# Second feed-forward product of a two-layer trunk: running sums kept in PSUM, four results in place of seven

## The chip, the core and the metric

The kernel runs on one core of one Trainium2 chip. The metric is device time in microseconds of one execution, as the median of several. The core has a matrix engine (TensorE, PE in the profile, with its weight loads as PEld), a vector engine (VectorE, DVE), a scalar engine (ScalarE, ACT), GpSimd (POOL) and a queue engine (SyncE, SP). TensorE writes to PSUM, which has 8 banks of 128 partitions x 512 fp32 numbers; VectorE and ScalarE read it. Each engine works through its own instructions in order and waits on semaphores for the others.

## The reference

Two layers on x of 512 tokens x 1024, each of attention and a feed-forward part, then a last norm:

```python
for l in range(DEPTH):                      # DEPTH = 2
    h = rmsnorm(x, attn_norm[l])
    proj = jnp.einsum('bsd,de->bse', h, w_in[l])
    ...
    x = x + jnp.einsum('bse,ed->bsd', mixed, w_o[l])
    h = rmsnorm(x, mlp_norm[l])
    u = jnp.square(jax.nn.relu(jnp.einsum('bsd,df->bsf', h, w_ff1[l])))     # 1024 -> 4096
    x = x + jnp.einsum('bsf,fd->bsd', u, w_ff2[l])                          # 4096 -> 1024
return rmsnorm(x, final_norm)
```

## The kernel before, in words

Every fp32 matrix is split into two parts, `hi` (rounded by ScalarE) and `lo` (the rest, by VectorE), and every product of two matrices is three matmuls, hi x hi, lo x hi and hi x lo (`three`, lines 261 to 266). The time goes in this order: attention of layer 0 (to about 243 us), feed-forward of layer 0 (to 569), the opening of layer 1 and its attention (to 812), feed-forward of layer 1 (to the end).

A feed-forward part runs over four groups of hidden columns (`for g in range(GROUPS)`, line 999), and each group holds two stages. The **first product** (lines 1002 to 1036) and the **second product** (lines 1037 to 1117) are both computed by a scheme of the Strassen kind: a 2 x 2 block product with seven block products and sums of blocks before and after. The first has seven steps named 1, 2, 5, 6, 7, 3, 4 (`HALVES`); it ends in activations F0 to F4. The second has seven steps, the `FORMS` 11, 21, x1, 22, x2, x3, x4. For each form:

- `roll` (line 906) splits one of the F tiles into Ah and Al, which are the stationary side of the matmuls. It is called two forms ahead; there are two buffers.
- `W.next("f")` hands out two weight units (128 x 1024 each, c = 0 and 1), each split into whi (ScalarE, line 122) and wlo (VectorE, line 123). `_Weights` keeps four pairs of such buffers in this part, so the split runs at most four units ahead.
- 24 matmuls of 512 columns go to two PSUM banks (r = 0 and 1, the two blocks of 128 tokens in one half of the tokens), in the order c, i, r: the banks take turns every three matmuls, and both are complete at the form's end (lines 1038 to 1052).
- `gather` (line 923) copies (first group, ScalarE) or adds (later groups, VectorE, line 929) both banks to that form's place in the SBUF tile Y, which has seven places of 128 x 1024.

The seven sums of products are put together in the last group only, in SBUF: `merge` (line 936) adds one place to another with an accumulating DMA from POOL's queue, `join` (line 933) does it on VectorE, `settle` (line 949) scales a result with its row factor r2 (on ScalarE in layer 0; on VectorE, with x turned by four transpositions added, in layer 1), and `add_to` (line 958) adds a scaled bank or place to a result. The result has four quarters, (token half i, column half j), each of two row blocks tb = 2i + r.

The weights of forms x1, x2, x3 and x4 are sums of weight blocks, made by DMA in HBM-to-SBUF accumulating transfers (`grow`, line 784, issued from POOL as line 789). `then` (line 792) ties each such DMA to the split of an earlier unit in the same buffer: the DMA for x4 is issued when x2's unit of the same c has been split; that for x2 when x1's has.

After the last form, layer 0 turns its result back (`back`, line 963: four transpositions on PE, an addition to x on VectorE, then `make_h`, one ScalarE and one VectorE instruction) and starts the first two products of layer 1 (`p`, lines 1129 to 1141). Layer 1 takes squares of its results (`square`), the root (`root`: VectorE, then a power on POOL), weighs with the norm's gains (`weigh`, or in `store`) and writes eight pieces of the output from SP's queue (line 992).

The order of instructions on each engine is that of a scheduler which fills in by priority, close to the order in which the code is written; `behind` (line 239) fixes one instruction after another. The bank tags are t (2 banks), mm (2), s (3) and o (1).

## Time and profile before

| | |
|---|---|
| median of 3 runs | 1148.61 us (1148.3 to 1149.41) |
| the profiled execution | 1148.57 us, of which the span from the first to the last instruction is 1146.5 us |
| TensorE busy | 1119.3 us, 98% of the span, 6834 matmuls |
| VectorE, ScalarE, GpSimd busy | 924.4, 722.1, 181.0 us |
| mean granted clock | 0.992 |

"L123" in a row is line 123 of the kernel. A group's row reads: line, engine, operation, what it writes <- what it reads, shapes, count. A row of a timeline reads: start, us, engine, line, operation, names, shape, count, and in brackets the engine's idle time just before it with what ended it. Names lose their buffer numbers, and the forms x1 to x4 all read as "x"; "f" are the banks of the first product, "q" and "yw" raw weights.

### The profile page before, as it was taken

To read this page: it belongs to the slowest core of one execution; us is meant where nothing else is said; L and a number is where in the kernel's file an instruction comes from. 1 tells how busy PE (TensorE), PEld (TensorE's weight loads), DVE (VectorE), ACT (ScalarE), POOL (GpSimd) and SP (SyncE) were. 2 spreads that over 40 slices of the span, in tenths; PEclk is the share of its full clock that TensorE was granted. 3 is DMA by queue.
4 is the path that set the end of the run, shared out by engine and by line. 5 is a ranking of instruction groups with operands and counts; after the bars stand their busy time and mean duration, and the time that the engine had idled before them with its cause. 6 is when DMAs were issued, how large, how long until landed. Compare 5 with 4: busy or idle time off the path is not lost.

```text
span 1146.5 us, 18089 instructions
## 1 busy us (share of the span) xinstructions
PE 1119.3 (98%) x6834; PEld 996.3 (87%) x6834; DVE 924.4 (81%) x1235; ACT 722.1 (63%) x1137; POOL 181.0 (16%) x261
## 2 busy tenths in 40 slices
PE   9999999999999999999899999999999999999995
PEld 6889989899899899898688898888998998988984
DVE  6898678898877878778869976887988788798697
ACT  6456666667867557565445566665678574675664
POOL 1001432110110201102000024231102011021022
PEclk9999999999999999999899999999999999999998
DMA  7664443346976885978416743524469859778595
GB/s 250 174 181 140 126 133 111 102 120 182 219 184 173 191 233 128 220 219 177 98 55 184 215 117 111 161 78 165 75 201 208 219 129 210 210 146 212 149 182 138
DMA packets 61479, 187.07 MB, mean 163 GB/s; under 512 B 7632, under 2 KB 8656, under 8 KB 61392
## 3 DMA queue, kind: packets, MB, share of 16 engines
q1 hardware_dynamic: 46416, 131.88, 36.2%
q0 software_dynamic: 14832, 54.01, 26.8%
q8 instruction: 54, 0.88, 0.3%
q14 instruction: 33, 0.27, 0.1%
q10 hardware_dynamic: 144, 0.02, 0.0%
HBM read 154.95 MB, written 2.10 MB: 137 GB/s over the span
## 4 chain that ended last, share of the span: by engine, by line
PE 82%; DVE 6%; issue 4%; DMA 3%; ACT 3%; POOL 1%; SPq 0%; POOLq 0%; ACTq 0%; DVEq 0%
PE f L264 8%; PE f L265 8%; PE f L266 8%; PE x L266 4%; PE x L264 4%; PE x L265 4%; PE wo L264 3%; PE wo L266 2%; PE wo L265 2%; DVE wlo L123 2%; DMA q<-in_w 2%; ACT whi L122 1%; PE T0s L539 1%; PE T1s L539 1%; PE v0w L264 1%
## 5 line engine op out<-in xcount | busy, mean ns | idle before, releaser
L123 DVE TENSOR_TENSOR wlo<-q,whi 128x1024 fp32r<-128x1024 f32 x184 | 223.3, 1221 | 69.5 <-ACT whi L122 69.3
L122 ACT ACTIVATE whi<-q 128x1024 fp32r<-128x1024 f32 x184 | 194.3, 1056 | 116.4 <-PE f L265 37.4
L266 PE MATMUL f<-T_hi,wlo 128*128 128x256 f32 x512 | 145.1, 283 | 0.7 <-DVE wlo L123 0.7
L264 PE MATMUL f<-T_hi,whi 128*128 128x256 f32 x512 | 145.0, 283 | 0.0
L265 PE MATMUL f<-T_lo,whi 128*128 128x256 f32 x512 | 144.9, 283 | 0.0
L264 PE MATMUL f<-h_hi,whi 128*128 128x256 f32 x384 | 109.7, 286 | 1.4 <-DVE F L896 1.4
L789 POOL DMA_DIRECT2D q<-in_w x64 | 56.3, 933 | 338.3 <-DVE wlo L123 306.3
L266 PE MATMUL f<-h_hi,wlo 128*128 128x256 f32 x384 | 108.6, 283 | 0.0
L265 PE MATMUL f<-h_lo,whi 128*128 128x256 f32 x384 | 108.6, 283 | 0.0
L264 PE MATMUL x<-whi,Ahx 128*128 128x512 f32 x256 | 100.9, 394 | 1.6 <-ACT Ahx L223 1.6
L266 PE MATMUL x<-whi,Alx 128*128 128x512 f32 x256 | 100.6, 393 | 1.3 <-DVE Alx L224 1.3
L265 PE MATMUL x<-wlo,Ahx 128*128 128x512 f32 x256 | 100.1, 391 | 0.0
L266 PEld LDWEIGHTS f<-T_hi,wlo 128*128 128x128 f32 x512 | 98.3, 192 | 1.1 <-DVE wlo L123 1.1
L264 PEld LDWEIGHTS f<-T_hi,whi 128*128 128x128 f32 x512 | 98.3, 192 | 0.0
L265 PEld LDWEIGHTS f<-T_lo,whi 128*128 128x128 f32 x512 | 98.3, 192 | 0.0
L123 DVE TENSOR_TENSOR wlo<-raw,whi 128x1024 fp32r<-128x1024 f32 (+1 forms) x68 | 79.2, 1171 | 7.7 <-ACT whi L122 7.6
L122 ACT ACTIVATE whi<-raw 128x1024 fp32r<-128x1024 f32 (+1 forms) x68 | 66.2, 982 | 29.7 <-PE p1d1q L265 5.3
L264 PEld LDWEIGHTS f<-h_hi,whi 128*128 128x128 f32 x384 | 73.5, 191 | 2.7 <-DVE F L896 1.8
L265 PEld LDWEIGHTS f<-h_lo,whi 128*128 128x128 f32 x384 | 73.6, 192 | 0.3
L266 PEld LDWEIGHTS f<-h_hi,wlo 128*128 128x128 f32 x384 | 73.6, 192 | 0.0
L264 PEld LDWEIGHTS x<-whi,Ahx 128*128 128x128 f32 x256 | 48.5, 189 | 11.9 <-ACT Ahx L223 2.0
L266 PEld LDWEIGHTS x<-whi,Alx 128*128 128x128 f32 x256 | 48.4, 189 | 11.8 <-DVE Alx L224 1.7
(965 smaller groups left out, 3108.7 us busy)
## 6 DMA issues: line engine op xcount, KB each, us to landing
q<-in_w SPq DMA_DIRECT2D x100, 512.0 KB, 4.6
q<-in_w POOLq DMA_DIRECT2D x84, 512.0 KB, 6.7
raw<-in_w SPq DMA_DIRECT2D x62, 512.0 KB, 3.7
yw<-in_w SPq DMA_DIRECT2D x12, 512.0 KB, 5.5
yw<-in_w POOLq DMA_DIRECT2D x12, 512.0 KB, 8.3
cs<-in_w SPq DMA_DIRECT2D x8, 512.0 KB, 7.5
ww<-in_w SPq DMA_DIRECT2D x8, 512.0 KB, 4.3
Y<-Y POOLq DMA_DIRECT2D x6, 512.0 KB, 6.1
```

What stands on the lines that cost most here:

```text
L122: h = nc.scalar.activation(hi[:, a:b], raw[:, a:b], AF.Copy)
L123: self.last = h, nc.vector.tensor_tensor(out=lo[:, a:b], in0=raw[:, a:b], in1=hi[:, a:b].bitcast(F32), op=ALU.subtract)
L264: nc.tensor.matmul(pt, ah, bh, start=first, stop=False, skip_group_check=onto)
L265: nc.tensor.matmul(pt, ah, bl, start=False, stop=False, skip_group_check=onto)
L266: nc.tensor.matmul(pt, al, bh, start=False, stop=last, skip_group_check=onto)
L539: nc.tensor.transpose(pt[:, n * P : (n + 1) * P], u["w"][qi][:, kb * P : (kb + 1) * P], ident)
L789: paced(nc.gpsimd.dma_start(t, quad(g, q, c), accum_op=ALU.add))
```

## The change

`TAPS` gives each form a chain and one of the four quarters. Form 11 opens chain r, 21 opens s, x1 opens t; 22 adds on to t's two banks, and x2, x3 and x4 add on to r's, whose sums so stay in PSUM from form 11 to the group's end. After every form the two banks, running sums by then, are read into the quarter that the form feeds: copied in the first group where it is the first to feed it, otherwise added. Y shrinks from seven places to four, and no merges, joins or copies between places are left. Within a form the loop is now r, c, i: all 12 matmuls of row block 0, its read, then those of row block 1. The row factor of layer 0 is applied in the last group as before; in layer 1 the factor is left out, and instead x, scaled with its inverse, is added to the quarters (`lay`) during the first products of groups 1 and 2, with the epsilon of the last norm scaled to match.

The place freed in SBUF goes to a fifth pair of split weights (pool f2 with three buffers, `pairs`), so the split runs up to five units ahead in the first product; in the second it is called four units ahead at a form's start and once more after its reads, and set behind them.

```diff
+TAPS = {"11": ("r", 1, 0), "21": ("s", 1, 0), "x1": ("t", 0, 1), "22": ("t", 1, 1),
+        "x2": ("r", 1, 1), "x3": ("r", 0, 1), "x4": ("r", 0, 0)}
...
+        if _UNITS[i][0] in "fq":
+            for x, y in zip(self.last, before):
+                self.behind(x, y)
+    def pairs(self):
+        return 3 * len(self.pools) - 1
...
-            self.do_split(i + 2 * len(self.pools), i)
+            self.do_split(i + self.pairs() - less, i)
...
-            Y = fp.tile([P, len(FORMS), 2, 512], F32, tag="Y", name=f"Y{l}")
+            Y = fp.tile([P, 2, 2, 2, 512], F32, tag="Y", name=f"Y{l}")
...
+            def gather(i, j, r, pt):
+                o = place(2 * i + r, j)
+                if 2 * i + j in fresh:
+                    nc.scalar.copy(o, pt)
+                    if r:
+                        fresh.discard(2 * i + j)
+                else:
+                    return nc.vector.tensor_add(o, o, pt)
...
+            def lay(tb, j):
+                o = place(tb, j)
+                n = 24 * j + tb
+                nc.vector.scalar_tensor_tensor(
+                    out=o, in0=turned(tb, j), scalar=fin[:, n : n + 1], in1=o, op0=ALU.mult, op1=ALU.add)
...
+                            if last and g in (1, 2) and q in "5673":
+                                lay("5673".index(q), g - 1)
+                chains = {}
                 for f, form in enumerate(FORMS):
+                    chain, i, j = TAPS[form]
+                    fresh_bank = chain not in chains
+                    if fresh_bank:
+                        chains[chain] = [bank(("s", "s", "s", "mm", "mm", "o")[2 * len(chains) + r], f"{form}{l}{g}{r}")
+                                         for r in range(2)]
+                    to = chains[chain]
+                    us = [W.next("f", 1 + c) for c in range(GP // 2)]
+                    hi, lo = rolled[form]
+                    for r in range(2):
+                        for n, (c, e) in enumerate((c, e) for c in range(GP // 2) for e in range(2)):
+                            at = 512 * c + 256 * e + r * P
+                            three(to[r], (hi[:, at : at + P], lo[:, at : at + P]), wpair(us[c], e, 512),
+                                  fresh_bank and n == 0, n == 3, not fresh_bank)
+                        tb = 2 * i + r
+                        if end and not last and form in ("21", "x2", "x3", "x4"):
+                            tapped = add_to(tb, j, to[r])
+                        else:
+                            tapped = gather(i, j, r, to[r])
...
+                            if form == "x4":
+                                for c_ in CAME[2 * r : 2 * r + 2]:
+                                    back(c_)
+                        elif form in ("21", "x2", "x3", "x4"):
+                            square(tb, j)
+                            if form in ("x2", "x4"):
+                                root(tb)
+                            if form in ("21", "x3"):
+                                weigh(tb, j)
+                            elif form == "x2":
+                                weigh(tb, 1)
+                                store(tb, 0, True)
+                                store(tb, 1, True)
+                            elif form == "x4":
+                                store(tb, 0, False)
+                                store(tb, 1, True)
                     if f + 2 < len(FORMS):
                         roll(FORMS[f + 2])
+                    if f + 1 < len(FORMS):
+                        had = W.split
+                        W.do_split(W.used + 3, W.used)
+                        if W.split > had and tapped:
+                            behind(W.last[1], tapped)
```

Left out of it are the removed lines of merges, joins and the old endings, and the place of the tile vs, which moves to a pool that is given back when attention ends.

How the instructions stand is shown at three places. The first is VectorE in group 1 of layer 0, forms x2 to x4. In the order before, from the roll (Alx) of x3 on: wlo are splits of weights, Alx rolls, and Y rows additions of a bank (first those of 22, then of x2, then of x3).

```order
L224 TENSOR_TENSOR Alx_4260<-F_2674,Ahx_4259 128x1024
L123 TENSOR_TENSOR wlo_4268<-q_0_2669,whi_4267 128x1024
L123 TENSOR_TENSOR wlo_4285<-q_0_2666,whi_4284 128x1024
L929 TENSOR_TENSOR Y_2860<-Y_2860,x_4265 128x512
L929 TENSOR_TENSOR Y_2860<-Y_2860,x_4266 128x512
L224 TENSOR_TENSOR Alx_4303<-F_2676,Ahx_4302 128x1024
L123 TENSOR_TENSOR wlo_4311<-q_0_2667,whi_4310 128x1024
L123 TENSOR_TENSOR wlo_4329<-yw_2862,whi_4328 128x1024
L929 TENSOR_TENSOR Y_2860<-Y_2860,x_4308 128x512
L929 TENSOR_TENSOR Y_2860<-Y_2860,x_4309 128x512
L123 TENSOR_TENSOR wlo_4349<-yw_2863,whi_4348 128x1024
```

The same place in the changed order, from the reads of 22 on (x_4178 and x_4179 are the banks of chain t, 11010 and 11011 those of chain r). Line numbers are the changed kernel's: 127 is the split, 234 the roll, 941 the addition.

```order
L941 TENSOR_TENSOR Y_2868<-Y_2868,x_4178 128x512
L941 TENSOR_TENSOR Y_2868<-Y_2868,x_4179 128x512
L127 TENSOR_TENSOR wlo_4255<-q_0_2672,whi_4254 128x1024
L234 TENSOR_TENSOR Alx_4251<-F_2678,Ahx_4250 128x1024
L127 TENSOR_TENSOR wlo_4260<-q_0_2673,whi_4259 128x1024
L941 TENSOR_TENSOR Y_2868<-Y_2868,11010_4098 128x512
L941 TENSOR_TENSOR Y_2868<-Y_2868,11011_4099 128x512
L127 TENSOR_TENSOR wlo_4295<-q_0_2670,whi_4294 128x1024
L234 TENSOR_TENSOR Alx_4291<-F_2680,Ahx_4290 128x1024
L127 TENSOR_TENSOR wlo_4301<-q_0_2671,whi_4300 128x1024
L941 TENSOR_TENSOR Y_2868<-Y_2868,11010_4098 128x512
L941 TENSOR_TENSOR Y_2868<-Y_2868,11011_4099 128x512
```

Before, a form's two reads stand together behind one or two splits that they do not depend on, and nothing on PE needs them soon. Now a split, a roll and a split stand between the second read of one form and the first read of the next, and the reads of x2 and x3 are from the banks that the next form adds to.

The second place is ScalarE in the last group of layer 0, from x2's roll to x3's. Before (L956 scales a result, L122 splits a weight, L223 rolls):

```order
L223 ACTIVATE Ahx_5711<-F_2675 128x1024
L122 ACTIVATE whi_5719<-q_0_2667 128x1024
L956 ACTIVATE Y_2860<-Y_2860,fin 128x512
L122 ACTIVATE whi_5736<-q_0_2668 128x1024
L956 ACTIVATE Y_2860<-Y_2860,fin 128x512
L223 ACTIVATE Ahx_5752<-F_2674 128x1024
L122 ACTIVATE whi_5761<-q_0_2669 128x1024
L122 ACTIVATE whi_5779<-q_0_2666 128x1024
```

and in the changed order (954 scales, 125 splits, 233 rolls):

```order
L125 ACTIVATE whi_5699<-q_0_2671 128x1024
L954 ACTIVATE Y_2868<-Y_2868,fin 128x512
L233 ACTIVATE Ahx_5690<-F_2679 128x1024
L954 ACTIVATE Y_2868<-Y_2868,fin 128x512
L125 ACTIVATE whi_5736<-q_0_2672 128x1024
L125 ACTIVATE whi_5740<-q_0_2673 128x1024
L954 ACTIVATE Y_2868<-Y_2868,fin 128x512
L233 ACTIVATE Ahx_5732<-F_2678 128x1024
```

Before, the first scaling reads a place that an accumulating DMA from POOL's queue writes. In POOL's order of that group before, L937 are those DMAs, Y to Y, among the weights' DMAs:

```order
L789 DMA q_0_2666<-in_w 128x1024
L937 DMA Y_2860<-Y_2860 128x1024
L789 DMA q_0_2667<-in_w 128x1024
L789 DMA q_0_2668<-in_w 128x1024
L789 DMA q_0_2669<-in_w 128x1024
L937 DMA Y_2860<-Y_2860 128x1024
L789 DMA q_0_2666<-in_w 128x1024
L789 DMA q_0_2667<-in_w 128x1024
L937 DMA Y_2860<-Y_2860 128x1024
```

In the changed order the scalings read places that VectorE has added to, and POOL's queue there holds weights' DMAs alone.

The third place is VectorE at the end of the program. Before, from the additions (L960) into the first quarter on; L977 is the first half of a root, L982 and L990 weigh:

```order
L960 SCALAR_TENSOR_TENSOR q_1_8430<-Y_8620,fin,q_1_8430 128x512 x2
L960 SCALAR_TENSOR_TENSOR Y_8620<-Y_8620,fin 128x512 x2
L960 SCALAR_TENSOR_TENSOR Y_8620<-x_11654,fin,Y_8620 128x512
L982 TENSOR_TENSOR Y_8620<-Y_8620,cs 128x512 x2
L977 TENSOR_SCALAR fin<-fin 128x1
L960 SCALAR_TENSOR_TENSOR Y_8620<-x_11655,fin,Y_8620 128x512
L990 SCALAR_TENSOR_TENSOR Y_8620<-Y_8620,fin,cs 128x512
L982 TENSOR_TENSOR q_1_8430<-q_1_8430,cs 128x512
L977 TENSOR_SCALAR fin<-fin 128x1
L990 SCALAR_TENSOR_TENSOR Y_8620<-Y_8620,fin,cs 128x512
```

In the changed order, from x3's reads on (941 adds a bank, 981 is the root's half, 986 and 994 weigh):

```order
L941 TENSOR_TENSOR Y_8590<-Y_8590,11130_11339 128x512
L941 TENSOR_TENSOR Y_8590<-Y_8590,11131_11340 128x512
L986 TENSOR_TENSOR Y_8590<-Y_8590,cs 128x512 x2
L941 TENSOR_TENSOR Y_8590<-Y_8590,11130_11339 128x512
L981 TENSOR_SCALAR fin<-fin 128x1
L994 SCALAR_TENSOR_TENSOR Y_8590<-Y_8590,fin,cs 128x512
L941 TENSOR_TENSOR Y_8590<-Y_8590,11131_11340 128x512
L981 TENSOR_SCALAR fin<-fin 128x1
L994 SCALAR_TENSOR_TENSOR Y_8590<-Y_8590,fin,cs 128x512
```

The additions of scaled places and of two banks with their factor are gone; what stands behind PE's last bank is one read, half a root and one weighing.

More of the change, by code (lines that the diff above doesn't have):

```diff
@@ L116, in split_part @@
             self.turn = k + 1
-            hi = self.pools[k // 2].tile([P, 1024], F32R, tag="whi", name=f"whi{i}")
-            lo = self.pools[k // 2].tile([P, 1024], F32R, tag="wlo", name=f"wlo{i}")
+            pool = self.pools[k > 1]
+            hi = pool.tile([P, 1024], F32R, tag="whi", name=f"whi{i}")
+            lo = pool.tile([P, 1024], F32R, tag="wlo", name=f"wlo{i}")
             self.tiles[i] = (hi, lo)
@@ L143, in do_split, with next @@
                 fn()
-    def next(self, kind):
+    def next(self, kind, less=0):
         i = self.used
@@ L241, in behind @@
             mybir.DependencyClass.NoSync, mybir.DependencyReason.DATA), reason="order")
+    W.behind = behind
     def rms_a(src, inv_n, col, name, floor=None):
@@ L1034, in trunk @@
                                 less(3, 1, 3)
-                            if end and q in "56":
-                                settle("56".index(q), 0)
+                            if last and g in (1, 2) and q in "5673":
+                                lay("5673".index(q), g - 1)
+                chains = {}
                 for f, form in enumerate(FORMS):
-                    to = [bank((("s", "s"), ("s", "mm"), ("mm", "o"))[f % 3][r], f"{form}{l}{g}{r}") for r in range(2)]
-                    work = [(c, i, r) for c in range(GP // 2) for i in range(2) for r in range(2)]
@@ new lines, in trunk @@
+                    for r in range(2):
[6 more added lines that the diff above has]
+                            tapped = add_to(tb, j, to[r])
+                        else:
+                            tapped = gather(i, j, r, to[r])
+                        if not end:
+                            continue
+                        if not last:
+                            if form in ("11", "x1", "22"):
+                                settle(tb, j)
+                            if form == "x1":
+                                settle(r, 0)
+                            if form == "x4":
[14 more added lines that the diff above has]
+                                store(tb, 1, True)
@@ L1131, in trunk @@
                 pts = [bank("mm", f"p{l + 1}{i}") for i in range(2)]
-                for tb in (0, 1):
-                    add_to(tb, 0, to[tb])
-                for c in CAME[2:4]:
-                    back(c)
                 for n, c in enumerate(CAME):
```

136 lines of the change are left out of this document (19 added, 117 removed).

## The prediction, made before the changed kernel ran

> **What bounds it now.** I read PE's share first, then the table of stages, then TensorE's own timeline for places where it stood still.
>
> ```profile
> PE 1119.3 (98%) x6834; PEld 996.3 (87%) x6834; DVE 924.4 (81%) x1235; ACT 722.1 (63%) x1137; POOL 181.0 (16%) x261
> 323.00:364.00 41.00, 41.00 (x343) 40.87 (x342) 29.41 (x30) 27.37 (x37) 3.50 (x4) 1.00 0.69 182
> 364.00:402.00 38.00, 38.00 (x170) 31.47 (x169) 33.39 (x36) 21.68 (x22) 7.12 (x8) 1.00 0.83 187
> 521.10:583.50 62.40, 57.26 (x250) 45.41 (x248) 52.31 (x63) 33.43 (x42) 8.07 (x11) 0.95 0.55 116
> 1090.80:1133.30 42.50, 41.32 (x194) 33.52 (x192) 38.10 (x45) 23.61 (x33) 9.77 (x13) 1.00 0.81 162
> ```
>
> The columns of a stage are its stretch, its length, then busy us (and instructions) of PE, PE's weight loads, DVE, ACT and POOL, then the granted clock, the DMA share and GB/s. The first stage is the first product of group 1 in layer 0, the second that group's second product. PE is busy in all of both: the middle of a feed-forward part is TensorE's own time, and removing DVE, ACT or DMA work there gains nothing. The third stage (last second product of layer 0 and the opening of layer 1) holds 5 us in which PE is not busy, at a mean clock of 0.95; the fourth is the last second product. The change keeps the number of matmuls and transposes, so it can gain only where PE stands still: here, behind PE's end, and at the two starts of a feed-forward part.
>
> ```profile
> 363.98 0.40 PE L264 MATMUL 11010_4097<-whi,Ah 128*128 128x512 f32 x1
> 396.64 0.39 PE L264 MATMUL x<-whi,Ahx 128*128 128x512 f32 x1
> ```
>
> These are the first matmuls of products 11 and x4 of one group, six products of 24 matmuls apart: 32.66 / 144 = 0.227 us a matmul, 5.45 us a product, 2.72 us for one of its two banks. This is my clock below; T is the start of a group's product 11.
>
> **Term 1, the end of layer 0.**
>
> ```profile
> 546.83 0.72 ACT L956 ACTIVATE Y<-Y,fin 128x512 f32<-128x512 f32 x1 [6.99 <-DMA Y<-Y]
> 548.11 0.39 PE L266 MATMUL x<-whi,Alx 128*128 128x512 f32 x1
> 550.12 0.50 PE L264 MATMUL x<-whi,Ahx 128*128 128x512 f32 x1 [1.62 <-ACT Ahx L223]
> 552.15 0.79 PE L266 MATMUL x<-whi,Alx 128*128 128x512 f32 x1 [1.30 <-DVE Alx L224]
> 552.74 0.63 PE L264 MATMUL x<-whi,Ahx 128*128 128x512 f32 x1
> 555.64 0.39 PE L265 MATMUL x<-wlo,Ahx 128*128 128x512 f32 x1
> 556.61 3.49 DVE L934 TENSOR_TENSOR Y<-Y 128x1024 f32<-128x1024 f32 x3
> 562.70 0.39 PE L266 MATMUL x<-whi,Alx 128*128 128x512 f32 x1
> 568.00 1.25 PE L966 MATMUL yT<-edge,Y 128*128 128x128 f32 x8 [1.89 <-DVE x L967]
> 573.55 1.03 PE L966 MATMUL yT<-edge,Y 128*128 128x128 f32 x8
> 574.34 0.71 PE L264 MATMUL p<-h_hi,whi 128*128 128x512 f32 x2
> 583.32 0.39 PE L266 MATMUL p<-h_hi,wlo 128*128 128x512 f32 x1
> ```
>
> ACT stands 6.99 us because the scaling of a result waits for a merging DMA; the roll of x3 (Ahx, Alx) is queued behind it, PE waits for both halves, and then matmuls come 0.43 us apart instead of 0.227 (552.74 on). From 548.11 to 555.64 there are 10 matmuls: 7.53 - 10 x 0.227 = 5.3 us lost. The merges and joins go with the change, so ACT has no DMA to wait for and the half-speed matmuls go too. From 562.70 to the end of the opening (583.32 + 0.23) there are 55 matmuls (12.5 us) and 32 transposes (eight take 574.34 - 573.55 = 0.79, so 3.2): 20.85 - 15.7 = 5.2 us lost, since DVE did 3.49 us of joins and then every addition to the last rows after the last matmul. Now rows 0 are added while PE computes rows 1, so two of the eight turns back come before PE's last half product. What is late next is the second weight of the opening: its split on DVE follows the last addition and two additions to x, some 3.3 us behind PE's end, while PE has 0.8 of transposes and 1.8 us of matmuls before it needs it: 0.7 us stays. The gain is 5.3 + 5.2 - 0.7 = **9.8 us**; at most 10.5, at least 5.3 if DVE is as late as now.
>
> **Term 2, the end of the kernel.**
>
> ```profile
> 1117.44 0.40 PE L266 MATMUL x<-whi,Alx 128*128 128x512 f32 x1
> 1119.02 0.66 PE L946 MATMUL xT<-edge,x 128*128 128x128 f32 x4 [1.18 <-DVE Y L952]
> 1132.93 0.39 PE L266 MATMUL x<-whi,Alx 128*128 128x512 f32 x1
> 1136.20 2.51 POOL L982 TENSOR_TENSOR q<-q,cs 128x512 f32<-128x512 f32 x1 [2.06 <-ACT F L972]
> 1138.45 0.63 ACT L972 ACTIVATE F<-Y 128x512 f32<-128x512 f32 x1
> 1138.99 0.19 ACT L972 ACTIVATION_READ_ACCUMULATOR F<-Y 128x1 f32 x1
> 1140.53 0.21 DVE L977 TENSOR_SCALAR fin<-fin 128x1 f32<-128x1 f32 x1
> 1140.81 0.54 POOL L978 TENSOR_TENSOR fin<-fin,mhalf 128x1 f32<-128x1 f32 x1 [1.59 <-DVE fin L977]
> 1141.39 0.75 DVE L990 SCALAR_TENSOR_TENSOR Y<-Y,fin,cs 128x512 f32<-128x512 f32 x1 [0.66 <-POOL fin L978]
> 1142.63 0.40 SPq L992 DMA_DIRECT2D out_xT<-q  x1
> ```
>
> PE loses 1119.02 - 1117.44 - 0.23 = 1.35 us where a transposition of x waits for a bank; these eight transpositions move into the first products of groups 1 and 2, where they cost PE what they cost it now. Behind PE's end (1133.32) the last output leaves at 1142.63: 9.3 us, in which one row block waits for a 2.5 us product on POOL and for DVE to work off four additions. After the change one addition (0.7), square and sum (0.75), root on DVE to POOL's start (0.3), power (0.55), weighing (0.8) and the second output's issue (0.45) are left: 3.6 us, plus 0.2 for the first reader and 0.4 because rows 0's weighing stands before it on DVE. That is 4.2, a gain of 5.1 + 1.35 = 6.5 us. Against it stand the weighings and squares that now come inside products 21, x2 and x3 (term 4): 1.6 us of waits. Net **4.9 us**, between 3 and 6.5.
>
> **Term 3, the starts of the first product.**
>
> ```profile
> 263.98 0.39 PE L266 MATMUL f<-T_hi,wlo 128*128 128x256 f32 x1 [0.33 <-DVE wlo L123]
> 273.61 0.39 PE L264 MATMUL f<-h_hi,whi 128*128 128x256 f32 x1 [0.72 <-DVE F L896]
> 832.84 0.38 PE L266 MATMUL f<-T_hi,wlo 128*128 128x256 f32 x1 [0.39 <-DVE wlo L123]
> 842.41 0.38 PE L264 MATMUL f<-h_hi,whi 128*128 128x256 f32 x1 [0.69 <-DVE F L896]
> ```
>
> With five pairs of split weights in place of four, the sums over two weights, and with them the DMAs that wait for them, are one weight (2.7 us) earlier. The four waits, 2.1 us, can all go; a burst on DVE could also add 1 us. I take **1.1 us**.
>
> **Term 4, the waits that the change adds.** Products x2, x3 and x4 now add into the same two banks, 22 into those of x1. Before PE may go on, DVE must have read a bank; behind that read, in order, stand two splits and a roll.
>
> ```profile
> 525.67 1.22 DVE L123 TENSOR_TENSOR wlo<-q,whi 128x1024 fp32r<-128x1024 f32 x1
> 526.80 1.22 DVE L914 SCALAR_TENSOR_TENSOR F<-F,F 128x1024 f32<-128x1024 f32 x1
> 529.07 0.68 DVE L929 TENSOR_TENSOR Y<-Y,11030_5589 128x512 f32<-128x512 f32 x1
> 529.67 0.68 DVE L929 TENSOR_TENSOR Y<-Y,11031_5590 128x512 f32<-128x512 f32 x1
> 390.01 1.06 ACT L122 ACTIVATE whi<-q 128x1024 fp32r<-128x1024 f32 x1 [2.26 <-DMA q<-in_w]
> 393.88 1.06 ACT L122 ACTIVATE whi<-q 128x1024 fp32r<-128x1024 f32 x1 [1.64 <-DMA q<-in_w]
> DMA to landing us min/median/max: 5.2/6.8/11.4
> ```
>
> DVE's starts are 1.13 us apart for 1024 columns and 0.60 for 512. From the end of one product to the first bank of the next being read it does one read, a split, a roll, a split, a read: 0.60 + 3 x 1.13 + 0.60 = 4.6, with 0.2 for the first reader 4.8, and PE comes back after 5.45. So 0.65 us is spare and DVE alone costs nothing; in the last group of layer 1, two weighings more (1.2) make it 6.0 behind 21 and, with two roots, 6.4 behind x2, so PE waits 0.55 + 0.95, the 1.6 above.
>
> But the roll follows the splits on ACT, and the split of x4's second weight waits for its accumulating DMA. After that landing come whi 1.05, Ahx 1.0, Alx 1.13, wlo 1.13 and the read 0.6: 5.0 us, due at T + 32.7, so it may land at T + 27.7. Now it lands at 393.8 - 364.0 = T + 29.8, and PE does not mind, since it waits for no read. In the new order x2's second split, which sends that DMA, comes behind the last read of x1 (T + 16.35 + 0.2 + 0.6), a split and a roll, and ends at T + 20.5; the issue is some 0.4 later, T + 20.9. A landing after 5.2 us costs nothing, after the median 6.8 nothing either (T + 27.7), after 11.4 it costs 4.6. Group 0 has fewer DVE additions and sends it earlier, group 3 loads nothing for a next group; groups 1 and 2 of both layers are exposed. I take the median with 0.4 us of scatter, 4 x 0.4 = **1.6 us lost**, between 0 and 18.
>
> **The sum.** The profiled execution took 1148.57 us, 2.1 more than its span of 1146.5, and 0.04 below the median of the three runs. 1148.57 - 9.8 - 4.9 - 1.1 + 1.6 = 1134.4.
>
> **Rivals.**
> *The late DMA stays late* (0.22). The transfers land where they do now, up to 2.1 us after T + 27.7, and PE waits before x4 in four groups, with some half-speed matmuls behind as at 552.74: 6 to 8 us in all, 1139 to 1141. For it: ACT waits for this DMA twice in the group shown. Against: the next group's loads, which share the DMA engines then, are sent later in the new order.
> *The cover is complete* (0.12). No new wait, all of terms 1 to 3: 10.5 + 6.5 + 2.1 = 19.1, so 1129.5.
> *It does not do what it says at layer 0's end* (0.05). ACT and DVE are late there without merges as well, since every scaling still stands in ACT's queue ahead of a roll: the gain of term 1 halves, 1139 to 1143.
> *Slower: the chains bind on the DMA* (0.04). PE waits at x4 for the read of its own bank, because DVE stands behind a roll and a split whose DMA is late. Terms 1 to 3 give 15.8; in the four exposed groups the waits outweigh that from 4 us each, that is with a transfer of 10.8 us; at 11.4 in all four, 18.4 us, 1151.
> *Slower: no cover inside a product* (0.02). PE shows the read of each of three continuations in eight groups, 24 x (0.2 + 0.6) = 19 us: 1152. Against it: 0.65 us is spare at each by the rows of term 4. The Trainium skill, page "Perfetto Trace Analysis", section "Matmuls", stands behind this case: it advises that independent matmul groups rotate through different PSUM banks, so that one's evacuation overlaps the next one's matmuls, and x2, x3 and x4 no longer rotate. In the trace of before, which does rotate, no wait of PE on such a read shows, so it neither proves nor denies the rule.
>
> My forecast, 1131.5 to 1138, has 0.55. The range of 1129.5 to 1142 takes in the late DMA and half the complete cover. Faster means by over 0.2% (2.3 us, what a measurement of this kernel can tell from no change): 0.90; within it 0.04; slower 0.06.
>
> **What would show it.** Term 1: no ACT wait for a DMA of Y, PE without a gap over 1 us from 521 to the end of the opening, a clock of 1.00 there, and a stage of about 53 us in place of 62.4. Term 2: last output issued some 4 us after PE's last matmul, the last second product near 40 us. Term 4: look at PE before the first matmul of x3 and x4 for waits on the read (L941 in the changed kernel), and on ACT for a wait on a DMA before x4's split. Waits of over 2 us there in most groups would prove me wrong, as would an unchanged gap where layer 1 opens.

## The result, and the profile after

The changed kernel takes 1156.05 us (median of 4 runs, 1154.85 to 1158.56) beside 1148.45 us for the kernel before: a ratio of 1.0068, 95% interval 1.0048 to 1.0087. It is slower by 0.7%, where 1134.4 us had been forecast. The forecast's gains are nearly all there; the waits that the change adds cost about 26 us in place of some 3.

TensorE's line of the page, and the four stages that answer to those shown of before (stretch, length, busy us of PE, weight loads, DVE, ACT and POOL, granted clock, DMA share, GB/s):

```profile
PE 1122.9 (97%) x6834; PEld 995.5 (86%) x6834; DVE 921.8 (80%) x1238; ACT 712.3 (62%) x1121; POOL 172.8 (15%) x253
324.30:365.18 40.88, 40.88 (x342) 40.78 (x340) 30.29 (x31) 26.84 (x36) 3.51 (x4) 1.00 0.78 200
365.18:403.50 38.32, 37.35 (x166) 30.53 (x165) 32.29 (x35) 20.82 (x22) 7.10 (x8) 1.00 0.74 168
525.23:579.61 54.38, 53.13 (x250) 43.51 (x248) 46.11 (x56) 33.07 (x42) 5.45 (x8) 1.00 0.43 94
1099.62:1147.76 48.14, 41.33 (x170) 32.89 (x168) 34.54 (x42) 24.83 (x37) 7.70 (x9) 0.93 0.52 117
```

The end of layer 0 fell from 62.4 to 54.4 us. But the second product of group 1, which was all PE's own time, now holds 1 us in which PE stands, and the last second product grew from 42.4 to 48.1 us at a clock of 0.93. PE's timeline shows the places; these four, among them the longest, stand in front of a continuation, a product that adds on to banks in use:

```profile
393.54 0.47 PE L276 MATMUL 11010_4098<-whi,Ahx 128*128 128x512 f32 x1 [0.97 <-DVE Y L941]
553.87 0.47 PE L276 MATMUL 11030_5572<-whi,Ahx 128*128 128x512 f32 x1 [1.25 <-DVE Y L964]
1052.04 0.47 PE L276 MATMUL 11120_10603<-whi,Ahx 128*128 128x512 f32 x1 [2.25 <-DVE Y L941]
1052.81 0.63 PE L276 MATMUL 11120_10603<-whi,Ahx 128*128 128x512 f32 x1
1053.24 0.63 PE L277 MATMUL 11120_10603<-wlo,Ahx 128*128 128x512 f32 x1
1139.76 0.77 PE L276 MATMUL 11130_11339<-whi,Ahx 128*128 128x512 f32 x1 [5.50 <-ACT Y L992]
```

The banks named 110.., 111.. are those of chain r: 393.54 and 553.87 are the first matmuls of x3, 1052.04 and 1139.76 of x4. Each waits for VectorE's read of the bank to which it adds. In the groups 0 PE also stops at 21, which opens a chain and waits for its roll: 0.70 us in layer 0, 0.94 and 0.70 in layer 1. Behind the longer two, matmuls come 0.43 us apart (1052.81 to 1053.24), as at 552.74 before.

The balance by stretches (us; T is the start of a group's product 11):

| stretch | before | after | early splits (below) |
|---|---|---|---|
| to T of group 0, layer 0 | 285.0 | 284.1 | 285.0 |
| groups 0, 1, 2 of layer 0 | 79.0, 78.6, 78.6 | 81.1, 79.9, 80.2 | 81.0, 78.6, 78.6 |
| last second product and opening | 62.4 | 54.4 | 52.7 |
| attention, to T of group 0, layer 1 | 270.2 | 270.6 | 271.1 |
| groups 0, 1, 2 of layer 1 | 79.0, 78.6, 79.4 | 84.5, 81.4, 83.5 | 84.7, 80.2, 78.6 |
| last second product | 42.4 | 48.1 | 39.8 |
| behind PE's last matmul | 13.3 | 7.4 | 8.0 |

In layer 1 the stretches of groups 0 and 1 each hold 1.6 us of transpositions that moved into the first products behind them (80.15 against 78.57 us in the early version); they left the last second product.

**Why a read is late.** Group 1 of layer 0 (T = 365.18), from the split of x3's second weight on, on ACT and on DVE:

```profile
388.39 1.06 ACT L125 ACTIVATE whi<-q 128x1024 fp32r<-128x1024 f32 x1 [1.47 <-DVE Y L941]
389.36 1.05 ACT L233 ACTIVATE Ahx<-F 128x1024 fp32r<-128x1024 f32 x1
390.44 1.23 DVE L234 TENSOR_TENSOR Alx<-F,Ahx 128x1024 fp32r<-128x1024 f32 x1 [0.33 <-ACT Ahx L233]
391.58 1.22 DVE L127 TENSOR_TENSOR wlo<-q,whi 128x1024 fp32r<-128x1024 f32 x1
392.71 0.68 DVE L941 TENSOR_TENSOR Y<-Y,11010_4098 128x512 f32<-128x512 f32 x1
```

The DMA that makes x3's second weight landed at 388.29 (T + 23.1), 0.1 us before ACT's split. From there to PE's first matmul of x3 at 393.54 it is 5.25 us: whi, roll on ACT, roll and split on DVE, read. x3 was due at T + 27.2. The bank itself had been complete since about 389.9, where its last matmul of x2 ended.

**Why the transfer is late.** POOL's issues in that group:

```profile
374.72 0.90 POOL L802 DMA_DIRECT2D q<-in_w  x1 [14.05 <-DVE wlo L127]
375.86 1.79 POOL L802 DMA_DIRECT2D q<-in_w  x2 [0.24 <-DVE Y L941]
380.71 0.88 POOL L802 DMA_DIRECT2D q<-in_w  x1 [3.06 <-DMA q<-in_w]
383.96 0.90 POOL L802 DMA_DIRECT2D q<-in_w  x1 [2.37 <-DVE wlo L127]
388.42 0.89 POOL L802 DMA_DIRECT2D q<-in_w  x1 [3.56 <-DVE Y L941]
```

These are the two sums for x2, the two for x3 and the two for x4, at T + 9.5, 10.7, 11.3, 15.5, 18.8 and 23.2. They land at T + 15.2, 18.1, 20.6, 23.1, 26.1 and 28.6, some 2.5 us apart, so a late first one makes all late. The fourth, x3's second, has one more tie: it waits on POOL for the first to land (the wait for a DMA in its row) and leaves 0.3 us later, here as in groups 1 and 2 of the traces of the kernel before, early splits, half late and late sums. Before the change the first left at T + 6.2 and landed at T + 11.8.

**In the last group** more comes behind a late transfer. ACT first, then DVE:

```profile
1131.98 1.06 ACT L125 ACTIVATE whi<-q 128x1024 fp32r<-128x1024 f32 x1 [2.75 <-DMA q<-in_w]
1132.95 0.62 ACT L976 ACTIVATE F<-Y 128x512 f32<-128x512 f32 x1
1133.56 1.04 ACT L233 ACTIVATE Ahx<-F 128x1024 fp32r<-128x1024 f32 x1
1133.69 0.27 DVE L981 TENSOR_SCALAR fin<-fin 128x1 f32<-128x1 f32 x1 [4.67 <-ACT F L976]
1134.63 1.23 DVE L234 TENSOR_TENSOR Alx<-F,Ahx 128x1024 fp32r<-128x1024 f32 x1
1137.01 0.27 DVE L981 TENSOR_SCALAR fin<-fin 128x1 f32<-128x1 f32 x1
1138.93 0.68 DVE L941 TENSOR_TENSOR Y<-Y,11130_11339 128x512 f32<-128x512 f32 x1
```

x4's second weight lands at T + 32.3. The square of x2's row block stands behind its split on ACT; DVE stands 4.67 us at the root that needs the square, and the roll of x4, a second root, weighings and a split follow before the read of x3's bank at 1138.93. PE's row at 1139.76 names a scaling of Y on ACT, which no matmul reads; the read of its bank ends at the same time, 1139.6.

### The profile page after: what moved, and what is told of

Same layout as the page of the kernel before. It is cut to its first block, busy times and chain, and to the rows that moved or that the text cites. A ratio compares the mean times of both kernels' runs of the same rounds, so it can differ in the third digit from the quotient of the medians.

```text
span 1155.2 us, 18065 instructions
## 1 busy us (share of the span) xinstructions
PE 1122.9 (97%) x6834; PEld 995.5 (86%) x6834; DVE 921.8 (80%) x1238; ACT 712.3 (62%) x1121; POOL 172.8 (15%) x253
## 4 chain that ended last, share of the span: by engine, by line
PE 67%; DMA 10%; DVE 10%; issue 6%; ACT 4%; POOL 2%; SPq 0%; POOLq 0%; ACTq 0%; DVEq 0%
DMA q<-in_w 9%; PE f L276 8%; PE f L277 8%; PE f L278 8%; DVE wlo L127 3%; PE wo L276 2%; PE wo L278 2%; PE wo L277 2%; DVE Alx L234 1%; DVE Y L941 1%; ACT whi L125 1%; POOL q L802 1%; ACT Ahx L233 1%; DVE F L926 1%; PE T0s L552 1%
## 5 line engine op out<-in xcount | busy, mean ns | idle before, releaser
L234 DVE TENSOR_TENSOR Alx<-F,Ahx 128x1024 fp32r<-128x1024 f32 x32 | 39.1, 1223 | 21.9 <-ACT Ahx L233 21.8
L896 ACT ACTIVATE F<-F 128x512 f32<-128x512 f32 x48 | 29.9, 625 | 23.7 <-DVE F L902 16.3
L897 ACT ACTIVATE F<-F 128x512 f32<-128x512 f32 x64 | 40.2, 629 | 1.4
L234 DVE TENSOR_TENSOR Al<-F,Ah 128x1024 fp32r<-128x1024 f32 x24 | 29.3, 1222 | 11.0 <-ACT Ah L233 11.0
L485 POOL TENSOR_TENSOR sig1s<-sig1s,C1s 128x128 f32<-128x128 f32 (+3 forms) x32 | 26.2, 819 | 70.1 <-DVE C1s L482 55.0
```

The source lines that it names most:

```text
L234: nc.vector.tensor_tensor(out=lo, in0=src, in1=hi.bitcast(F32), op=ALU.subtract)
L485: nc.gpsimd.tensor_mul(sig[:, 0:wd], sig[:, 0:wd], C[:, 1 : wd + 1])
L896: nc.scalar.activation(f(n), f(n) if src is None else src, AF.Relu, scale=scale)
L897: nc.scalar.activation(f(n), f(n), AF.Square)
```

## The experiments

Each kernel is the changed one, or the version with early splits, with the edits shown.

### What makes PE wait

**Fresh banks.** Where PE waits for a read, does the shared bank make the wait, or the late weight itself?

```diff
-                    fresh_bank = chain not in chains
+                    fresh_bank, chain = True, "rst"[f % 3]
...
-    chains[chain] = [bank(("s", "s", "s", "mm", "mm", "o")[2 * len(chains) + r], f"{form}{l}{g}{r}")
+    chains[chain] = [bank(("s", "s", "s", "mm", "mm", "o")[2 * (f % 3) + r], f"{form}{l}{g}{r}")
```

> Every form starts in the pair of banks that was read longest ago (three pairs take turns) and adds to nothing; the order of instructions on every engine stays that of the changed kernel. Left out of the computation: the running sums over forms. Theory 1 (late weights through shared banks): in the changed kernel the second weights of x3 and x4 come late, VectorE stands behind their roll and split, so the read of a bank comes late, and PE waits only because the next form adds to that same bank. Then no wait of PE on a read (L941) is left at x3 and x4, the last second product falls from 48.1 us to about 43, and the time from 1156 to about 1141 to 1145. Theory 2 (late weights by themselves): PE would wait for the split or the roll anyway, at the same places and almost as long; 1153 to 1156.

Measured: 1144.61 us (1141.58 to 1151.31, ten runs). Two stages of it, group 1 of layer 0 and the last second product:

```profile
365.00:402.00 37.00, 37.00 (x165) 30.62 (x163) 31.59 (x35) 20.86 (x22) 6.46 (x8) 1.00 0.73 166
1090.80:1136.60 45.80, 41.54 (x169) 33.02 (x168) 34.92 (x42) 25.09 (x37) 7.68 (x9) 0.93 0.54 122
```

In the middle group PE no longer stands, with every instruction in its old order and x3's second weight as late as before (T + 22.8 to 24.6 in groups 1 and 2). So there the shared bank turns a late weight into a wait. In the last group PE still waits, 1.55 us for x4's roll and 1.9 us for a split: 45.8 us, not 43, so there the weight is late by itself too.

The Trainium skill, page "Perfetto Trace Analysis", section "Matmuls", advises that independent groups rotate through PSUM banks. This run agrees with it (11.4 us better with banks that rotate); the version with early splits shows that it isn't the whole rule, since chained banks cost nothing in its groups 1 and 2 (78.6 us).

**Single blocks.** Is it the transfers that are late, or is VectorE's queue too long in itself?

```diff
                 else:
-                    paced(nc.gpsimd.dma_start(t, quad(g, q, c), accum_op=ALU.add))
                     W.raw[_AT[("f", l, g, form, c)]] = t
```

> The changed kernel without the accumulating DMAs of the second product: each form takes the block that already lies in its place, rolls and splits it as before. Left out of the computation: the sums of weight blocks of x1, x2, x3 and x4. Theory 1 (late weights): no ACT wait on a DMA before the splits of x3 and x4, VectorE reads in time, and PE's waits at x3 and x4 vanish: middle groups lose some 9 us of waits, the last one 5 or more, 1138 to 1144. Rival (VectorE's own queue: read, split, roll, split, read is too long beside a product in itself): the waits of about 1 us at x3 and x4 of each group stay, 1150 to 1155.

Measured: 1132.66 us, less than expected.

```profile
362.47:400.20 37.73, 37.73 (x169) 31.23 (x168) 32.69 (x35) 21.51 (x22) 1.75 (x2) 1.00 0.29 79
1081.10:1121.60 40.50, 38.58 (x170) 31.17 (x168) 34.44 (x42) 24.69 (x37) 2.42 (x3) 1.00 0.13 45
```

With the same order on VectorE and nothing to wait for, all middle groups run as before the change (78.6 us, without the moved transpositions). VectorE's queue does fit beside a product, as the prediction had it; 0.8 us before 22 and 1.4 us before x4 of the last group are left. The groups 0 lose nothing either (79.0 us, and 80.6 with 1.6 of transpositions), so what they lose in the changed kernel hangs on the transfers too.

### When the sums leave

**Early splits.** The look-ahead is called at a form's start again, so that the splits of x1, and the sums that follow them, don't stand behind the reads.

```diff
-                    us = [W.next("f", 1 + c) for c in range(GP // 2)]
+                    us = [W.next("f") for c in range(GP // 2)]
...
-                    if f + 1 < len(FORMS):
-                        had = W.split
-                        W.do_split(W.used + 3, W.used)
-                        if W.split > had and tapped:
-                            behind(W.last[1], tapped)
```

> The split of the form after next's first weight is called at a form's start again, not behind its reads; still five pairs. Theory 1: x2's first accumulating DMA leaves about 5 us earlier than T + 9.5, and the four behind it with it, so that x3's second weight lands by T + 20 in place of T + 23.1 and x4's by T + 26 in place of T + 28.6 to 32.3. The waits of the middle groups go, that of the last is halved: 1141 to 1147. Rival: the transfers are limited by their own queue (2.5 us each) or by slots that PE still reads, and come hardly earlier: within 2 us of 1156; or the reads now stand behind more splits: above 1157.

Measured: 1138.60 us, ratio 0.9919 (0.9904 to 0.9934): this is faster than both kernels. x2's first sum leaves at T + 3.1 and x3's second lands at T + 18.3 to 20.2 in groups 1 and 2. Those groups lose nothing (first row), and the end of layer 0 takes 52.7 us without a stop (second):

```profile
365.97:403.80 37.83, 37.83 (x169) 31.35 (x168) 32.77 (x35) 21.74 (x22) 7.11 (x8) 1.00 0.87 189
523.10:575.80 52.70, 52.70 (x250) 43.67 (x248) 46.01 (x56) 33.03 (x42) 5.46 (x8) 1.00 0.47 98
```

**Late sums, half late.** The reverse: splits and reads stay early, and only the DMAs for x2 and x3 wait longer, by one product or by one weight.

```diff
-                    then("f", g, "x1", c, grow, g, "x2", "22", c)
+                    then("f", g, "22", c, grow, g, "x2", "22", c)                    # late sums
+                    then("f", g, "22" if c else "x1", 1 - c, grow, g, "x2", "22", c) # half late
...
-                            then("f", g, "x1", c, grow, g, "x3", "22", c_)
+                            then("f", g, "22", c, grow, g, "x3", "22", c_)           # late sums
+                            then("f", g, "22", 0, grow, g, "x3", "22", c_)           # half late
```

> The version with early splits (1138.6 us), but the accumulating DMAs for x2 and x3 are tied to the splits of 22 in place of those of x1, one product (5.45 us) later; splits, reads and rolls stand where they stood. Theory 1: x2's first sum leaves near T + 8.5 in place of T + 3.1, x3's second lands after T + 23 in place of T + 18.3 to 20.2, ACT waits for it and PE waits for the reads of x2 and x3 again, as in the changed kernel: 1146 to 1158. Rival (the place of the reads on VectorE, not the transfers, made the early version fast): within 2 us of 1138.6.

> The version with early splits, with the accumulating DMAs for x2 and x3 one weight (2.7 us) later in place of one product. Theory 1 with its bound for x3's second weight (landing by T + 22, since whi, roll, split and read behind it take 5.2 us and x3 is due at T + 27.2): it lands at T + 21 to 22.5, so PE's wait before x3 is under 0.5 us in groups 1 and 2, and the time between the early version's 1138.6 and the changed kernel's 1156, near the lower end: 1139 to 1146. Rival (cost grows in proportion to lateness, 38 us for 5.45 us): half of that, 1155 or more.

Measured: 1176.65 us for late sums and 1156.97 us for half late. Both directions were right, both sizes too small, and half late took the time that its rival had named (1155 or more). The DMA row shows what happened. It is the mean busy share of the DMA engines in 1 us slices from T of group 1 of layer 0, in tenths: first the changed kernel, then early splits, then late sums.

```profile
DMA  8582000000098999999999997999997880888999
DMA  9874739919699999999999997894757396999997
DMA  9865000000009699999999999999999935887999
```

```profile
GB/s 340 147 303 98 0 0 0 0 0 0 0 74 147 213 197 201 209 201 221 205 209 209 197 197 143 131 209 205 365 356 307 156 356 12 160 332 115 160 193 168
```

In the changed kernel and in late sums the engines stand idle from T + 4 until the first sum leaves, and are full from then on, at some 200 GB/s (the row below them is the changed kernel's), that is about 2.5 us for a weight of 512 KB. An idle stretch can't be made up. The four traces together, for groups 1 and 2 of both layers:

| | x3's second weight lands at T + | stop before x3, us |
|---|---|---|
| early splits | 20.2, 18.7, 18.3, 18.6 | none |
| half late | 22.6, 21.5, 22.4, 23.6 | 1.1, 0, 0.8, 2.0 |
| changed kernel | 23.1, 23.1, 22.8, 22.7 | 1.1, 1.1, 0.8, 0.7 |
| late sums | 24.0, 25.6, 23.6, 25.6 | 2.3, 4.1, 2.7, 4.0 |

The stop is about the landing less 22, and up to 1.1 us more in these groups, so the bound of T + 22 held there. The whole time grew in proportion all the same, as the rival had it: 18.4 us for sums sent 2.7 us later and 38 us for 5.45. What failed in the half-late forecast was the landing: it came up to 1.1 us later than expected, as late as in the changed kernel. And the first and last groups were in neither sum: the groups 0 took 85.1 and 86.0 us in half late against 81.0 and 84.7 with early splits, and its last group stood 2.7 us behind x1; in late sums the stretch at the end of layer 0 took 59.3 us.

### What else the change moved

**Late ending.** x2's squares, root, weighing and outputs behind the reads of x3, in the changed kernel; and then the same edit with early splits and four pairs of split weights (four late), and with early splits, five pairs and the shorter look-ahead of group0_four below (combined).

```diff
-                            if form in ("x2", "x4"):
-                                root(tb)
...
+                    if end and last and form == "x3":
+                        for tb in (2, 3):
+                            square(tb, 1)
+                            root(tb)
+                            weigh(tb, 1)
+                            store(tb, 0, True)
+                            store(tb, 1, True)
```

> In the last group of layer 1 squares, root, weighing and outputs of x2's two row blocks are called behind the reads of x3; nothing else is moved. Theory 3: there x4's roll and last split stand on VectorE behind two roots and weighings that wait for squares on ACT, and this makes the 5.7 us wait of PE before x4 and the half-speed matmuls behind it (2.9 us). Then PE waits about 2 us at most there, at full speed, and the end of the kernel behind PE grows by 1 us at most: 1147.5 to 1150. Rival: x4's weight, landed at T + 32.3, sets that wait, and the moved work only filled it: a wait of 3 us or more stays, the tail grows by 1 to 3 us, 1152 to 1156.

Measured: 1159.09 us (1154.04 to 1160.44), above both forecasts and not clearly apart from the changed kernel's 1154.85 to 1158.56. The edit's own place gained: the last second product took 44.5 us in place of 48.1, with 2.6 us of PE's wait before x4 left of 5.5 and the same time behind PE (7.5 us), though x4's second weight landed 0.8 us earlier in this trace (T + 31.5). But 8 matmuls at half speed came behind it, and the six groups ahead, whose instructions weren't touched, lost 3 us more in this trace than in the changed kernel's. So by these two traces the moved work made up to half of that wait and x4's late weight the rest, and the total doesn't show it.

**Four pairs.** Early splits with four pairs in place of five.

```diff
-        return 3 * len(self.pools) - 1
+        return 2 * len(self.pools)
...
-            f2 = right.enter_context(tc.tile_pool(name=f"f2{l}", bufs=3, side="right"))
+            f2 = right.enter_context(tc.tile_pool(name=f"f2{l}", bufs=2, side="right"))
```

> The version with early splits, with four pairs of split weights as before the change. Theory: each split and each sum's DMA is one weight (2.7 us) later than with five pairs, still earlier than in the changed kernel; the waits at the starts of the first product come back (0.9 us in layer 0, up to 1 in layer 1), and x4's second weight, needed at T + 27.7, lands at T + 27 to 28.5, so that x4 costs up to 1 us in four groups: 1140 to 1144. Rival: the fifth pair carries the whole gain of the early version: 1150 or more.

Measured: 1140.00 us, as expected in sum, not in its parts. The first wait at the start of the first product is back (0.7 us in layer 0, 0.8 in layer 1). Middle groups lose nothing, the groups 0 run at 79.0 us (80.6 less 1.6 in layer 1) where five pairs took 81.0 and 84.7, and the last one stands 3.0 us before x4 though no split there waits for a DMA:

```profile
1116.54 3.22 POOL L982 TENSOR_TENSOR fin<-fin,mhalf 128x1 f32<-128x1 f32 x1 [8.47 <-DVE fin L981]
1119.79 0.72 ACT L992 ACTIVATE Y<-Y,fin 128x512 f32<-128x512 f32 x1 [3.08 <-POOL fin L982]
```

ACT waits for the power on POOL with a weighing, the second square stands behind it, the second root behind that, and the read of x3's bank behind the root.

> Four pairs, early splits, and squares, root, weighing and outputs of x2's row blocks behind the reads of x3. With four pairs PE waited 3.0 us before x4, where no DMA was late: VectorE's read stood behind the second root, that behind a square on ScalarE, and that behind two weighings that waited for the power on GpSimd (3.2 us). Theory 3: this wait goes, and the end behind PE grows by 1 us at most: 1137 to 1138.5 against 1140.0. Rival: the work comes back at the end: 1139.5 or more.

Measured: 1136.41 us, ratio 0.9896 (0.9879 to 0.9913), the best of the kernels that leave nothing out. The last second product fell from 45.8 to 40.6 us, and the time behind PE grew by 0.6. Here, without late weights, the moved ending carried the whole wait.

> Early splits, four weights of look-ahead in the first groups and five elsewhere, and x2's ending behind the reads of x3. With five pairs no wait is left before x4, so the moved ending should change nothing beside the run without it (within 1.5 us of it): 1131 to 1136. If theory 3 holds for any timing it is not slower; rival: the moved squares and weighings stand before x4's own on ScalarE and the tail grows by 1.5 us or more.

Measured: 1140.24 us. Beside the same kernel without the moved ending (group0_four, 1138.83) that is no difference beyond their spread, as it should be; both came out above their forecast, by what the groups 0 still lost.

**The groups 0.** With five pairs and early splits, PE stops at 21 in the first group of each layer, and before x3 in layer 0. Two tries to remove it:

```diff
+                    us = [W.next("f")]                              # roll_first
+                    if g == f == 0:
+                        for late, early in zip(W.last, turns["21"]):
+                            behind(late, early)
+                    us.append(W.next("f"))
...
+                    us = [W.next("f", int(g == 0)) for c in range(GP // 2)]   # group0_four
```

> The version with early splits, and in the first group of each layer the split of x1's first weight is put behind the roll of 21 on ScalarE and VectorE. Theory 4: in that group the split stands ahead of the roll and waits 2.4 us for a DMA that lands at T + 3.7 to 4.1, and PE waits for the roll at the start of 21 (0.4 + 0.7 us in layer 0, 1.4 + 0.7 us and 1.6 us of half-speed matmuls in layer 1). Then these go, all but 0.3 us: about 1134.5, between 1133 and 1136. Rival: the roll is late because its own F tile is late (ACT's activations), so nothing or under 1 us comes: 1137.5 to 1139.

> The version with early splits, with a look-ahead of four weights in the second product of the first group of each layer and of five elsewhere. Theory 4, corrected by the last runs: in that group it is the fifth split ahead that puts a wait for a DMA before the rolls of 21 and of x1 on ScalarE; with four pairs the group took 79.0 us in layer 0 and with five 81.0 (80.6 against 84.7 in layer 1). Then both groups run as with four pairs: 1138.6 - 2.0 - 4.1, about 1132.5, between 1131 and 1135. Rival: the group's copies and squares on ScalarE move the wait elsewhere again, as in the run before: 1136 to 1139.

Measured: 1138.81 us (1134.60 to 1140.67) and 1138.83 us (1137.90 to 1140.26): both above their forecasts, as their rivals had it. In the first the stop at 21 went, and stops before x3 came, 2.0 us in layer 0 and 1.0 in layer 1. In the second the scheduler still put the split ahead of the roll of 21:

```profile
287.06 1.06 ACT L125 ACTIVATE whi<-q 128x1024 fp32r<-128x1024 f32 x1 [1.65 <-DMA q<-in_w]
288.03 0.62 ACT L897 ACTIVATE F<-F 128x512 f32<-128x512 f32 x1
288.68 1.06 ACT L233 ACTIVATE Ah<-F 128x1024 fp32r<-128x1024 f32 x1
```

That four pairs free these groups is measured; which of the moved instructions does it was not separated.

**Both banks last.** Early splits with the loop of before inside a form.

```diff
-                    for r in range(2):
-                        for n, (c, e) in enumerate((c, e) for c in range(GP // 2) for e in range(2)):
+                    for n, (c, e) in enumerate((c, e) for c in range(GP // 2) for e in range(2)):
+                        for r in range(2):
```

> The version with early splits with the loops in the order of before, weights outside and row blocks inside, so that both banks of a form are complete only at its end. Theory 5 (the row blocks' order is what covers the reads): PE waits about 0.8 us (0.2 + 0.6) before 22, x3 and x4 of all eight groups, 19 us, and the ends of layer 0 and of the kernel lose the 2 to 3 us of overlap each: 1157 to 1163. Rival: what precedes the read on VectorE sets the wait, and the order of the row blocks is worth little: 1139 to 1145.

Measured: 1155.08 us, 16.5 us slower than with row blocks. Measured start to start, the waits in groups 1 and 2 are 0.54 us before 22 and 0.45 before x4, less than 0.8, and 0.54 to 1.46 before x3; the end of layer 0 takes 56.9 in place of 52.7 us, more than expected. The order by row blocks is what hides the reads.

## Why the prediction failed, by its own steps

*Term 1, the end of layer 0: right.* Forecast -9.8 us, a stage of about 53. Measured 54.4, of which 1.4 is a wait before x3 (term 4), and 52.7 in the version with early splits, where that wait is gone. ACT has no wait for a DMA of Y there, the clock is 1.00, and 0.4 + 0.9 us stay where layer 1's next product starts.

*Term 2, the end of the kernel: right behind PE.* Forecast 4.2 us from PE's end to the last output's issue; PE ends at 1147.76, and the last of these four leaves at 1151.96:

```profile
1150.79 0.75 DVE L994 SCALAR_TENSOR_TENSOR Y<-Y,fin,cs 128x512 f32<-128x512 f32 x1 [0.66 <-POOL fin L982]
1148.41 3.94 SPq L996 DMA_DIRECT2D out_xT<-Y  x4
```

The last four outputs leave in this group of issues, of which one takes 0.4. The term's other half, 1.6 us of waits in the last group, was priced on VectorE's queue alone. The squares' place on ACT behind a split that waits for a DMA was not followed; that group lost 10 us (48.1 against 42.4 - 1.35 - 3.2 = 37.8).

*Term 3, the starts: near right at its four waits.* The two of 0.33 and 0.39 us went, the other two, 0.72 and 0.69, stayed at 0.62 each: 0.9 us of the 1.1. Over whole stretches it is -0.9 us in layer 0 and +0.4 in layer 1, which one trace doesn't settle: the same stretch of layer 0 took 283.5 to 285.2 us in the traces with five pairs.

*Term 4: this step failed*, at 26 us in place of 1.6 + 1.6: 5.0 in groups 0 to 2 of layer 0, 1.4 in its last, 9.2 (12.4 less the 3.2 of moved transpositions) in groups 0 to 2 of layer 1, and 10.3 in the last. "DVE alone costs nothing" held (single blocks). What went wrong was the other half, "x4's second weight ... may land at T + 27.7. [...] I take the median":

- The same 5 us stand behind x3's second weight, which so had to land by T + 22. Only x4's was set against its bound; x3's was put at nothing without a reason. In the trace of before, x3's landed at T + 21.4 to 23.4 in these groups, so two of four were late already, unseen because PE read no bank then.
- The issue of x4's second sum was put at T + 20.9; it came at T + 22.9 to 23.4 in groups 1 and 2, since x2's second split waits for x2's own second sum, which landed at T + 17.7 to 18.1 in place of 16.3 to 16.6, behind a first one that now left 3.3 us later. A median time from issue to landing (6.8) hides that sums behind one another land 2.5 us apart.
- Group 0 was left out because it sends x4's second sum earlier. It did (T + 20.9 and 21.6), but the sum landed at T + 29.1 and 31.3, and with the stops at 21 and x4 these groups lost 2.1 us in layer 0 and 3.9 in layer 1.
- No price was put on a stop beyond its length. In these traces stops of about 2 us and more bring 6 to 12 matmuls at half speed, 1.2 to 2.4 us more.

The rival "the chains bind on the DMA" (0.04, 1151 us) named the mechanism and priced it by x4 alone. That its 1151 us came near the measured time is partly luck: it left out x3, the groups 0 and the last group of layer 1.

## What to carry to other kernels

A buffer that the next product adds to gives each continuation a due time: work back from it through every queue to the transfer behind it, for each continuation, and set the landing of before against it, late ones that nobody waited for included. When an edit puts work behind reads, ask which DMAs that work sends, and whether the DMA engines stand idle until then. An ending that is worked off during the last products belongs behind the read that PE needs next.

## What the runs showed of the hardware that wasn't expected

*Half speed after short stops.* In the traces of this study, 19 of the 20 stops of PE of 1.97 to 5.7 us in the feed-forward parts and the opening of layer 1 (start to start, less the matmul's own 0.227) were followed by 6 to 12 matmuls 0.43 us apart, beginning 0.3 to 1.6 us after the stop's end; of shorter stops only three pairs within 4 us were (1.38 + 0.69, 1.59 + 0.69, 1.78 + 1.47), and a pair of 1.58 + 0.70 was not. The Trainium skill, page "TensorE: Matmul & The Clock Gate", section "Part 1: The HAM clock gate", gives an idle window of about 3.4 us; here 2 us were enough in 19 of 20 places.

*A power on GpSimd beside VectorE.* The 128x1 power took 0.54 us wherever VectorE stood idle, 0.57 to 1.00 in most places beside a busy VectorE, 1.39 in one, 2.08 us in four traces and 3.22 (row above) in one. What makes the long ones is not shown: in the long ones VectorE worked on without a gap, but so it did beside one of 0.94 us in the changed kernel (at 1137.36). The Trainium skill, page "SBUF — State Buffer", section "SBUF: two separate sides", says that a GpSimd instruction that reads SBUF and a VectorE one with two SBUF inputs lock each other out for a whole instruction; the direction of the rows agrees, the differences between them it doesn't explain.

*Scatter of transfers.* The same instructions in groups 0 to 2 took 490.6 us in the changed kernel's trace and 493.6 in that of late ending. The times of kernels with such waits spread by 4 to 6 us over four runs; those of the kernel before spread by 1.4 here, but by 2.7 to 5.4 in the sets run beside the experiments. That a wait on a DMA without slack also varies more is likely, and not shown.
